# Projection weights on ScalarE's queue, later stores of rotated parts, squares on ScalarE and a new attention order in a two-layer hybrid kernel

## The chip, the cores and the metric

The kernel runs on one core of a Trainium2 chip. The metric is the device time of one execution in microseconds (us); the time before is the median of three executions.

## What is computed

The reference takes 1024 latent tokens of width 1024 (on a grid 64 wide), 256 context tokens and conditioning vectors, and returns the latent stream after two layers. All is float32. Cut to what matters here:

```
layer 0:  u = LN0(h)*(1+scale)+shift            # adaptive values: matrix x conditioning vector
          conv path:  three 512-column projections of u, a gated convolution of width 3
          attention:  q, k = u @ w_qk, rotated by 2-D rotary angles; keys also from 256 context rows
                      4 heads, each (softmax(q1 k1') - lam*softmax(q2 k2')) @ v
                      each head's output o is scaled by rsqrt(mean(o*o) + eps)
          h = LN(alpha*h + gate * ([conv, attention] @ w_out)),  then a squared-ReLU MLP
layer 1:  grouped 2-D Fourier mixing, then a squared-ReLU MLP
```

## The kernel before

A float32 product is made from three matmuls (`mm3`, L87 to L89): each operand is kept as a rounded high part and a low part, the remainder. `split` makes them: a cast on ScalarE (L97) for the high part, a subtraction on VectorE or GpSimd (L98) for the low part. The program's engine order is the order in which the Python code issues instructions; each engine runs its own list in order and waits on semaphores where it needs another's result. A tile from a pool has as many buffers as `bufs` says, and its next use waits until the old one is read. In the built program the DMAs issued by SyncE (SP) and ScalarE take eight semaphores in turn, counted over both engines, and each DMA waits until the one eight before it has landed.

The span of the profiled execution falls into these stretches:

- 0 to 107 us: modulations and the value projection.
- 107 to 265 us: the eight q/k projections. Each loads one weight tile of 128x1024 (512 KB, tag `wraw`, two buffers) with `w_load`, makes its parts `wh` and `wl` with `w_parts`, and multiplies two blocks of 512 columns (for K also one of 256, the context). A pair of projections (A, B) gives one rotated result: `rotate` (L413) combines both blocks with cosine and sine tables on VectorE, GpSimd and ScalarE and makes four parts `rp0` to `rp3` (tags with two buffers), which are stored in DRAM (`Qd`, `Kd`) for the attention to read. `store(*keep)` issues the stores waiting in a list until as many are left as it has arguments.
- 265 to 401 us: twelve conv projections (c = 0 to 11), with weights from the same series: projection i calls `next_weights(i)`, which loads the weights of i+2 and splits those of i+1. So a conv weight loaded late holds up the split behind it.
- Among both runs `Ada`, the adaptive values: eight loads `wa` from `in_ada_w` (L152, SP) for each of eight units, a VectorE instruction on each, and at the end of a unit a load of `in_ada_b` (L177).
- 401 to 672 us: attention. Sixteen pairs of query tiles (four pairs for each of four heads) go through a pipeline in which each step has a number in the table `PIPE`; sorting (number + pair) gives one order for all engines. The steps: S scores of a tile and a half c (PE, L614 to L618; c = 0 and 1 use different k tiles), M row maximum (VectorE L621), E exponential (ScalarE L626), CB, PD, PE the combination of both softmaxes (VectorE L631, GpSimd L635 and L638), T transposes of two key blocks (PE L652), H and L the parts of the transposed weights (ScalarE L658, VectorE L663), P six matmuls into `po` (mm3), OC copy of `po` to `OT` (ScalarE L675), SQ squares (GpSimd L680), SS sums of the squares (PE, L684), SC their use (VectorE). `po` has one buffer in PSUM.
- 672 to 2394.5 us: output projection, layer norms, MLPs and Fourier mixing.

Of the kernel before, what the change touches and what calls it, by code (L numbers as in the profile page):

```python
# [13 lines left out]
F32R = mybir.dt.float32r  # L14
AF = mybir.ActivationFunctionType
ALU = mybir.AluOpType
# [4 lines left out]
P = 128  # L21
# [9 lines left out]
FS = 1.0 / math.sqrt(1024.0 * 128.0)  # L31


def raw(ap):
    return ap.bitcast(F32)


def body(tc, nc, I, O, dbg=None):
# [10 lines left out]
    def popen(name, **kw):  # L49
        p = tc.alloc_tile_pool(name=name, bufs=kw.pop("bufs", 1), **kw)  # L50
        pools[name] = p
        return p

    def pclose(*names):
        for n in names:
            pools.pop(n).release()
# [39 lines left out]
    def split(hi, lo, src, eng=None):  # L96
        a = nc.scalar.copy(hi, src)  # L97
        return a, (eng or nc.vector).tensor_tensor(out=lo, in0=src, in1=raw(hi), op=ALU.subtract)  # L98
# [115 lines left out]
    wsrc = [I["w_qk"][i] for i in range(8)] + [I["w_cv"][i] for i in range(12)]  # L214
    wraws, wtiles = {}, {}

    def w_load(i):
        if i < len(wsrc):
            wraws[i] = pW.tile([P, D], F32, name="wraw", tag="wraw")
            nc.sync.dma_start(out=wraws[i], in_=wsrc[i])  # L220

    def w_parts(i):
        if i < len(wsrc):
# [137 lines left out]
    def store(*keep):  # L361
        while len(stores) > len(keep):
            for o, i in stores.pop(0):
                nc.sync.dma_start(out=o, in_=i)
# [36 lines left out]
    def next_weights(i):  # L401
        w_load(i + 2)
        if i:
            w_parts(i + 1)
# [6 lines left out]
        return ps  # L411

    def rotate(pR, ada, pA, pB, c, dst, scale):  # L413
        parts = [pR.tile([P, 512], F32R, name=f"rp{i}", tag=f"rp{i}", bufs=2) for i in range(4)]
        t = [pR.tile([P, 512], F32, name=f"rt{i}", tag=f"rt{i}") for i in range(4)]
        nc.vector.tensor_tensor(out=t[0], in0=pA, in1=cosT[:, c], op=ALU.mult)
        nc.vector.tensor_tensor(out=t[2], in0=pB, in1=sinT[:, c], op=ALU.mult)
        nc.vector.tensor_tensor(out=t[1], in0=pA, in1=sinT[:, c], op=ALU.mult)
        nc.vector.tensor_tensor(out=t[3], in0=pB, in1=cosT[:, c], op=ALU.mult)
        nc.gpsimd.tensor_tensor(out=t[0], in0=t[0], in1=t[2], op=ALU.subtract)  # L420
        nc.gpsimd.tensor_tensor(out=t[1], in0=t[1], in1=t[3], op=ALU.add)
        ada.tick()
        for i in range(2):
            if scale is None:
                split(parts[i], parts[2 + i], t[i])
            else:
                nc.scalar.mul(parts[i], t[i], scale)
                nc.vector.scalar_tensor_tensor(out=parts[2 + i], in0=t[i], scalar=scale, in1=raw(parts[i]),
                                               op0=ALU.mult, op1=ALU.subtract)
        return [(dst[:, i, :, c], raw(parts[i])) for i in range(4)]  # L430
# [51 lines left out]
    heads = {}  # L482
# [29 lines left out]
    pR = popen("pR", bufs=2, side="left", **tile_waits)  # L512
    pAda = popen("pAda", side="left", **tile_waits)
    with tc.manual_schedule(engines={mybir.EngineType.PE, mybir.EngineType.DVE, mybir.EngineType.Activation,
                                     mybir.EngineType.Pool, mybir.EngineType.SP}):
        w_load(2)
        cosT = pR.tile([P, N], F32, name="cosT", bufs=1)
        sinT = pR.tile([P, N], F32, name="sinT", bufs=1)
        nc.sync.dma_start(out=cosT, in_=I["rope_cos"])
        nc.sync.dma_start(out=sinT, in_=I["rope_sin"])  # L520
        ada = Ada(pAda, ada0[:4])
        for hp in range(2):
            for which in range(2):
                iA = hp * 4 + which * 2
                if iA:
                    next_weights(iA)
                blks = [(UH[b], UL[b], 512) for b in range(2)] + [(CH, CL, NC)] * which
                psA = []
                for blk in blks:
                    psA.append(proj(iA, *blk))  # L530
                    ada.tick(2)
                next_weights(iA + 1)
                dst = (Kd if which else Qd)[hp]
                for b, blk in enumerate(blks):
                    pB = proj(iA + 1, *blk, "tr")
                    if b < 2:
                        st = rotate(pR, ada, psA[b], pB, slice(b * 512, b * 512 + 512), dst, None if which else 0.125)
                    else:
                        parts = [pR.tile([P, 512], F32R, name=f"rp{i}", tag=f"rp{i}", bufs=2) for i in range(4)]
                        split(parts[0][:, :NC], parts[2][:, :NC], psA[b][:, :NC])  # L540
                        split(parts[1][:, :NC], parts[3][:, :NC], pB[:, :NC])
                        st = [(dst[:, i, :, N:NK], raw(parts[i][:, :NC])) for i in range(4)]
                    stores.append(st)
                    store(0)
                    ada.tick()
        ada.tick(len(ada0) * KT)
        ada.end()
        store()
        pclose("pAda", "pR", "pUc")
        pC = popen("pC", bufs=1, side="right", **tile_waits)  # L550
        cb = [pC.tile([P, 514], F32, name=f"cb{i}") for i in range(2)]
        for b in range(2):
            nc.gpsimd.memset(cb[b][:, 0:1], 0.0)
        ada = Ada(popen("pAda", side="right", **tile_waits), ada0[4:])
        pHv = None
        for c in range(12):
            i = 8 + c
            cv = Conv(c)
            next_weights(i)
            for b in range(2):  # L560
                cv.Y(b)
            for b in range(2):
                ps = proj(i, UH[b], UL[b], 512, ("mm", "tr")[b])
                ada.tick(2)
                cv.V(b, ps)
                cv.O(b)
                store(0)
            if c == 7:
                ada.tick(len(ada0) * KT)
            if c == 8:  # L570
                ada.end()
                pclose("pAda")
                popen("pHqL", side="left", **tile_waits)
                pHv = popen("pHv", bufs=2, side="left", **tile_waits)
                load_set(0)
                load_v(0)
                load_set(1)
        store()
# [61 lines left out]
    class Pair:  # L640
# [34 lines left out]
            nc.scalar.copy(heads[self.h]["OT"][:, self.qp * 256:(self.qp + 1) * 256], self.po[:, 0:256])  # L675

        def SQ(self):
            oc = heads[self.h]["OT"][:, self.qp * 256:(self.qp + 1) * 256]
            self.sq = pA.tile([P, 256], F32, name="sq", tag="sq", bufs=1)
            nc.gpsimd.tensor_tensor(out=self.sq, in0=oc, in1=oc, op=ALU.mult)  # L680

        def SS(self):
            for j in range(2):
# [145 lines left out]
    for n in range(3, 8):  # L829
        m = n - 3  # L830
# [4 lines left out]
    for h in range(4):  # L835
        k = PIPE["SC",] + 4 * h + 3
        at(k + 0.001, lambda h=h: finish_stats(h))
        if h < 3:
            for m in range(4):
                base = k + 0.6 + m // 2 * 0.8  # L840
                fr = base + (PIPE["FR",] - base) % 1.0
                fs, fl = (fr + PIPE[o,] - PIPE["FR",] for o in ("FS", "FL"))
                for t, f in ((fr, finish_rows), (fs, finish_split), (fl, finish_low)):
                    at(t + 0.0001 * m, lambda f=f, h=h, m=m: f(h, m))
                written[h] = fl + 0.001
# [360 lines left out]
    T = tail["T"]  # L1206
# [237 lines left out]


PIPE = {
    ("X",): -9.6372,
    ("FR",): -9.5434,
    ("FS",): -8.8084,
    ("FL",): -7.9375,  # L1450
    ("S", 1, 0): 0.0000,
    ("M", 1, 0): 0.3034,
    ("S", 0, 0): 0.3526,
    ("E", 1, 0): 0.4332,
    ("M", 0, 0): 0.4777,
    ("S", 1, 1): 0.5700,
    ("E", 0, 0): 0.6075,
    ("M", 1, 1): 0.6724,
    ("S", 0, 1): 0.7592,
    ("CB", 0): 0.7920,  # L1460
    ("E", 1, 1): 0.8163,
    ("PD", 0): 0.8428,
    ("M", 0, 1): 0.8874,
    ("E", 0, 1): 1.0180,
    ("PE", 0): 1.0297,
    ("CB", 1): 1.1548,
    ("PD", 1): 1.2721,
    ("PE", 1): 1.3784,
    ("T", 0): 1.6732,
    ("H", 0): 1.7224,  # L1470
    ("L", 0): 1.7858,
    ("T", 1): 1.8624,
    ("H", 1): 1.9242,
    ("L", 1): 1.9812,
    ("T", 2): 2.0461,
    ("P", 0): 2.0852,
    ("H", 2): 2.0977,
    ("P", 1): 2.1431,
    ("L", 2): 2.1548,
    ("T", 3): 2.2197,  # L1480
    ("H", 3): 2.2690,
    ("L", 3): 2.3292,
    ("P", 2): 2.3511,
    ("T", 4): 2.4089,
    ("H", 4): 2.4660,
    ("L", 4): 2.5231,
    ("P", 3): 2.5684,
    ("P", 4): 2.7576,
    ("OC",): 2.8491,
    ("SQ",): 2.8874,  # L1490
    ("SS",): 2.9515,
    ("SC",): 2.9891,
}

PERM = np.concatenate([np.arange(512), [512], 1024 - np.arange(1, 512)])
# [109 lines left out]
```

## Time and profile before

| what | value |
|---|---|
| median of three executions | 2397.02 us (2391.02 to 2400.21) |
| profiled execution, own time | 2396.29 us |
| its span | 2394.5 us |
| mean granted TensorE clock | 0.968 |
| busy in the span | PE 2220.9 us (93%), VectorE 1255.8 (52%), GpSimd 1025.7 (43%), ScalarE 695.3 (29%) |

The page gives the busy time of each engine, and for slices of the span the granted TensorE clock as a share of full speed. A timeline gives single instructions, with the idle time of the engine ahead of them and what ended it. DMA share is the mean busy share of the core's 16 DMA engines.

### The profile page before, as it was taken

The page shows a single profiled execution, that of the slowest core. Times are in us where ns is not written, and L with a number is a line of the kernel's source. Part 1 is how long each engine was busy: PE and PEld are TensorE (multiplying, and loading weights), DVE is VectorE, ACT ScalarE, POOL GpSimd, SP SyncE. Part 2 cuts the span into 40 slices and gives each one's busy share as a digit, 9 for nine tenths or more (in the row PEclk, how much of TensorE's full clock was granted, in tenths as well). Part 3 has the DMA queues.
Part 4 walks back from the last instruction along what each step waited for, and adds up shares of the span by engine and source line. Part 5 has one row for each costly group of instructions (what it writes and reads, how often), then busy time and mean ns, then how long its engine had stood idle before and what let it go on. Part 6 is the DMA issues. An engine that isn't in the chain of part 4 may idle for free.

```text
span 2394.5 us, 26145 instructions
## 1 busy us (share of the span) xinstructions
PE 2220.9 (93%) x9978; PEld 1791.4 (75%) x9978; DVE 1255.8 (52%) x1751; ACT 695.3 (29%) x1039; POOL 1025.7 (43%) x704
## 2 busy tenths in 40 slices
PE   7988697887888999999999999898999999999998
PEld 3766585777777877777788887666787888888886
DVE  7545562677545676665443434646544334434335
ACT  5311111666535221112222213435421121121122
POOL 3432222777625433233356643737634233233241
PEclk9998898999899999999999999999999999999999
DMA  7344538354146343332223313345311111111111
GB/s 297 142 149 143 187 127 220 81 128 116 45 123 209 111 157 116 110 115 94 87 97 106 127 49 111 128 156 180 106 61 45 44 54 44 49 49 44 53 44 70
DMA packets 121869, 261.98 MB, mean 109 GB/s; under 512 B 14642, under 2 KB 44594, under 8 KB 121488
## 3 DMA queue, kind: packets, MB, share of 16 engines
q1 hardware_dynamic: 120704, 254.69, 32.8%
q0 software_dynamic: 1040, 5.62, 0.7%
q8 instruction: 78, 1.28, 0.2%
q14 instruction: 47, 0.39, 0.1%
HBM read 213.06 MB, written 47.21 MB: 109 GB/s over the span
## 4 chain that ended last, share of the span: by engine, by line
PE 61%; DMA 12%; POOL 8%; DVE 8%; issue 5%; ACT 2%; SPq 2%; POOLq 0%; DVEq 0%; ACTq 0%
PE bky L87 10%; PE bky L88 10%; PE bky L89 9%; PE bkh L89 8%; PE bkh L88 8%; PE bkh L87 8%; DMA wa<-in_ada_w 3%; DVE aacc L160 2%; DMA wa<-in_ada_b 1%; DMA Kd<-rp 1%; DMA k<-Kd 1%; PE pj L89 1%; PE pj L87 1%; PE pj L88 1%; POOL ra L889 1%
## 5 line engine op out<-in xcount | busy, mean ns | idle before, releaser
L1014 DVE TENSOR_TENSOR acc<-bky,acc 128x512 f32<-128x512 f32 x448 | 304.4, 688 | 323.7 <-PE bky L89 323.1
L87 PE MATMUL bky<-wh,hh 128*128 128x512 f32 x1024 | 404.6, 396 | 18.8 <-DVE acc L1014 15.6
L88 PE MATMUL bky<-wl,hh 128*128 128x512 f32 x1024 | 403.6, 394 | 0.0
L89 PE MATMUL bky<-wh,hl 128*128 128x512 f32 x1024 | 402.2, 393 | 0.0
L998 POOL TENSOR_TENSOR hl<-r,hh 128x512 fp32r<-128x512 f32 x128 | 179.0, 1401 | 409.0 <-DVE r L997 400.0
L961 ACT CAST wh<-wraw 128x1024 fp32r<-128x1024 f32 x128 | 131.4, 1049 | 677.2 <-PE bky L89 482.0
L962 POOL TENSOR_TENSOR wl<-wraw,wh 128x1024 fp32r<-128x1024 f32 x56 | 137.5, 2460 | 303.2 <-ACT wh L961 303.2
L997 DVE TENSOR_TENSOR r<-r 128x512 f32<-128x512 f32 x128 | 118.5, 932 | 243.8 <-ACT hh L996 240.1
L87 PEld LDWEIGHTS bky<-wh,hh 128*128 128x128 f32 x1024 | 193.5, 189 | 70.1 <-DVE acc L1014 22.8
L88 PEld LDWEIGHTS bky<-wl,hh 128*128 128x128 f32 x1024 | 193.6, 189 | 43.3 <-issue 0.7
L89 PEld LDWEIGHTS bky<-wh,hl 128*128 128x128 f32 x1024 | 193.6, 189 | 42.7
L88 PE MATMUL bkh<-UB,wh 128*128 128x512 f32 x512 | 201.1, 393 | 0.7 <-POOL UB L133 0.7
L87 PE MATMUL bkh<-UB,wh 128*128 128x512 f32 x512 | 200.8, 393 | 0.0
L89 PE MATMUL bkh<-UB,wl 128*128 128x512 f32 x512 | 200.8, 393 | 0.0
L960 POOL TENSOR_TENSOR wraw<-wraw,gateg 128x1024 f32<-128x1024 f32 x64 | 156.0, 2439 | 97.8 <-DMA wraw<-in_w 90.3
L87 PE MATMUL bkh<-UA,wh 128*128 128x512 f32 x448 | 177.9, 397 | 0.0
L88 PE MATMUL bkh<-UA,wh 128*128 128x512 f32 x448 | 176.3, 394 | 0.0
L89 PE MATMUL bkh<-UA,wl 128*128 128x512 f32 x448 | 175.7, 394 | 0.0
L160 DVE SCALAR_TENSOR_TENSOR aacc<-wa,cs,aacc 128x512 f32<-128x512 f32 x140 | 143.7, 1027 | 37.5 <-DMA wa<-in_ada_w 35.2
L87 PE MATMUL pj<-UH,wh 128*128 128x512 f32 x320 | 132.5, 414 | 33.1 <-ACT wh L97 33.1
L962 DVE TENSOR_TENSOR wl<-wraw,wh 128x1024 fp32r<-128x1024 f32 x72 | 117.0, 1632 | 81.1 <-ACT wh L961 81.0
L995 ACT ACTIVATE r<-bkh 128x512 f32<-128x512 f32 x120 | 70.7, 595 | 294.8 <-PE bkh L89 283.5
(386 smaller groups left out, 4252.2 us busy)
## 6 DMA issues: line engine op xcount, KB each, us to landing
wraw<-in_w SPq DMA_DIRECT2D x128, 512.0 KB
wa<-in_ada_w SPq DMA_DIRECT2D x160, 256.0 KB
xt<-in_ada_w SPq DMA_DIRECT2D x16, 512.0 KB
xt<-in_x SPq DMA_DIRECT2D x16, 512.0 KB
acc<-Hd SPq DMA_DIRECT2D x16, 512.0 KB
wraw<-in_w_cv SPq DMA_DIRECT2D x12, 512.0 KB
aa<-Ad SPq DMA_DIRECT2D x16, 384.0 KB
k<-Kd SPq DMA_DIRECT2D x16, 320.0 KB
```

What stands on the lines that cost most here:

```text
L87: nc.tensor.matmul(ps, aH, bH, start=start, stop=False)
L88: nc.tensor.matmul(ps, aH, bL, start=False, stop=False)
L89: nc.tensor.matmul(ps, aL, bH, start=False, stop=stop)
L160: nc.vector.scalar_tensor_tensor(out=acc[0], in0=wa, scalar=cs[:, k, 0:1], in1=acc[0], op0=ALU.mult, op1=ALU.add)
L889: nc.gpsimd.tensor_scalar(r, r, 1.0 / D, eps, ALU.mult, ALU.add)
L960: nc.gpsimd.tensor_tensor(out=w, in0=w, in1=g, op=ALU.mult)
L961: nc.scalar.copy(wh, w)
L962: eng.tensor_tensor(out=wl, in0=w, in1=raw(wh), op=ALU.subtract)
L995: nc.scalar.activation(r, ps, AF.Relu)
L997: nc.vector.tensor_tensor(out=r, in0=r, in1=r, op=ALU.mult)
L998: pace[0] = nc.gpsimd.tensor_tensor(out=hl[:, c], in0=r, in1=raw(hh[:, c]), op=ALU.subtract)
L1014: pace[1] = nc.vector.tensor_tensor(out=a[:, c], in0=ps, in1=a[:, c], op=ALU.add)
```

## The change

Four edits. `w_load` issues the weight loads on ScalarE instead of SP. The four `rp` tags get three buffers instead of two, and in the q/k projections the stores of a rotated block are issued two blocks later than its rotation (`store(0, 1)` keeps two entries, `store(0)` kept one); in the conv loop the list is emptied after the first block instead of all but one after each. SQ becomes a Square activation on ScalarE that reads `po` from PSUM, instead of a product on GpSimd that reads `OT`. The table `PIPE` has new numbers, and the four finishing steps FR of a head go in two pairs one period (0.45 for the last) apart instead of all in one place.

```
-            nc.sync.dma_start(out=wraws[i], in_=wsrc[i])
+            nc.scalar.dma_start(out=wraws[i], in_=wsrc[i])
...
-        parts = [pR.tile([P, 512], F32R, name=f"rp{i}", tag=f"rp{i}", bufs=2) for i in range(4)]
+        parts = [pR.tile([P, 512], F32R, name=f"rp{i}", tag=f"rp{i}", bufs=3) for i in range(4)]
...
-                    store(0)
+                    store(0, 1)
...
-                store(0)
+                if not b:
+                    store()
...
         def SQ(self):
-            oc = heads[self.h]["OT"][:, self.qp * 256:(self.qp + 1) * 256]
             self.sq = pA.tile([P, 256], F32, name="sq", tag="sq", bufs=1)
-            nc.gpsimd.tensor_tensor(out=self.sq, in0=oc, in1=oc, op=ALU.mult)
+            nc.scalar.activation(self.sq, self.po[:, 0:256], AF.Square)
...
-                base = k + 0.6 + m // 2 * 0.8
-                fr = base + (PIPE["FR",] - base) % 1.0
+                base = k + 0.6
+                fr = base + (PIPE["FR",] - base) % 1.0 + m // 2 * (1 if h < 2 else 0.45)
...
-    ("P", 3): 2.5684,
-    ("P", 4): 2.7576,
-    ("OC",): 2.8491,
-    ("SQ",): 2.8874,
-    ("SS",): 2.9515,
+    ("P", 3): 2.5668,
+    ("P", 4): 2.7686,
+    ("OC",): 2.8469,
+    ("SQ",): 2.8749,
+    ("SS",): 2.9703,
```

**ScalarE, from the last K rotation into the second conv projection.** Before, casts of weights (`wh`), of rotated parts (`rp`) and copies of the conv gate (`gs`) follow each other:

```order
L97 CAST rp_1727<-rt_1731 128x512
L97 CAST rp_1728<-rt_1732 128x512
L97 CAST rp_1775<-rt_1779 128x512
L97 CAST rp_1776<-rt_1780 128x512
L97 CAST rp_1822<-pj 128x256
L97 CAST rp_1823<-pj 128x256
L97 CAST wh<-wraw 128x1024
L442 COPY gs<-pj 128x512 x2
L97 CAST wh<-wraw 128x1024 x2
```

In the changed program the loads stand among them:

```order
L97 CAST rp_1818<-pj 128x256
L97 CAST rp_1819<-pj 128x256
L220 DMA wraw<-in_w_cv 128x1024
L97 CAST wh<-wraw 128x1024
L442 COPY gs<-pj 128x512 x2
L220 DMA wraw<-in_w_cv 128x1024
L97 CAST wh<-wraw 128x1024
L220 DMA wraw<-in_w_cv 128x1024
L97 CAST wh<-wraw 128x1024
L476 CAST coh_2064<-cy_2023 128x512
L476 CAST coh_2113<-co 128x512
```

The first load here is for conv projection 2, the next for 3 (it stands ahead of the cast of the weights of 2), the last for 4. Each load stands ahead of a cast of other weights, and whatever holds the load up holds up that cast. By the eight semaphores the load for projection 3 waits until the third of the 17 `wa` loads shown below has landed.

**SP, the last stores of K and what follows.** Before:

```order
L177 DMA wa<-in_ada_b 128x512
L364 DMA Kd_961<-rp_1822 4x32x256
L364 DMA Kd_961<-rp_1823 4x32x256
L364 DMA Kd_961<-rp_1824 4x32x256
L364 DMA Kd_961<-rp_1825 4x32x256
L364 DMA G2d_955<-wa 1x512
L152 DMA wa<-in_ada_w 128x512 x7
L220 DMA wraw<-in_w_cv 128x1024
L152 DMA wa<-in_ada_w 128x512 x4
L220 DMA wraw<-in_w_cv 128x1024
```

In the changed program:

```order
L364 DMA Kd_961<-rp_1777 4x32x512
L364 DMA Kd_961<-rp_1818 4x32x256
L364 DMA Kd_961<-rp_1819 4x32x256
L364 DMA Kd_961<-rp_1820 4x32x256
L364 DMA Kd_961<-rp_1821 4x32x256
L364 DMA G2d_955<-wa 1x512
L152 DMA wa<-in_ada_w 128x512 x17
L364 DMA Ad_962<-coh_2064 128x512
L364 DMA Ad_963<-cy_2023 128x512
L152 DMA wa<-in_ada_w 128x512 x4
```

The weight loads are gone from between the `wa` loads. Earlier in this list the stores of the first two Q blocks now stand together behind 22 `wa` loads and the first `in_ada_b` load; before, the first block's stores stood behind 14 `wa` loads.

**PE, the end of one pair of attention.** The names: `s` scores, `pt` transposes, `po` output. Before, the last row of P4, then the scores of c = 1 of a later pair's first tile, the last transposes T1 of the next pair, and SS:

```order
L89 MATMUL po<-ph,vs_2611 128x256
L614 MATMUL s_3256<-k_2614,q 128x512
L615 MATMUL s_3256<-k_2615,q 128x512
L614 MATMUL s_3256<-k_2614,q 128x512
L615 MATMUL s_3256<-k_2615,q 128x512
L617 MATMUL s_3256<-k_2614,q 128x256
L618 MATMUL s_3256<-kx,q 128x256
L652 MATMUL pt<-ident,e_3079 128x128
L652 MATMUL pt<-ident,e_3139 128x128
L652 MATMUL pt<-ident,e_3079 128x128
L652 MATMUL pt<-ident,e_3139 128x128
L684 MATMUL po<-ones,sq 128x1 x2
```

In the changed program the same place:

```order
L619 MATMUL s_3250<-kx,q 128x256
L87 MATMUL po<-ph,vs_2609 128x256
L88 MATMUL po<-pl,vs_2609 128x256
L89 MATMUL po<-ph,vs_2611 128x256
L87 MATMUL po<-ph,vs_2609 128x256
L88 MATMUL po<-pl,vs_2609 128x256
L89 MATMUL po<-ph,vs_2611 128x256
L653 MATMUL pt<-ident,e_3085 128x128
L653 MATMUL pt<-ident,e_3146 128x128
L653 MATMUL pt<-ident,e_3085 128x128
L653 MATMUL pt<-ident,e_3146 128x128
L684 MATMUL po<-ones,sq 128x1 x2
```

The scores stand ahead of P4 now, and P4 directly ahead of T1 and SS. The same exchange was made with P3 and the group of scores before these (S11), so that the order from S11 to SS is S11, P3, T0, S01, P4, T1, SS where it was S11, T0, P4, S01, T1, SS. On ScalarE `sq<-po` stands right behind `OT<-po`, ahead of the next cast `ph<-pt`.

## Rows read from the trace of the kernel before

**Rows 1.** Windows by stage: start:end length, busy of each engine, PEclk, DMA share.

```profile
107.00:265.00 158.00, 131.56 (x584) 106.09 (x582) 70.36 (x89) 20.97 (x31) 42.20 (x26) 0.93 0.45 156
265.00:401.00 136.00, 118.19 (x489) 94.86 (x490) 71.52 (x112) 17.86 (x23) 34.34 (x17) 0.91 0.60 173
401.00:672.00 271.00, 222.41 (x1333) 194.95 (x1331) 174.69 (x255) 153.47 (x247) 178.62 (x104) 0.91 0.42 109
```

**Rows 2.** Waits, 107 to 401 us: sum, times, longest.

```profile
ACT wh L97 <- DMA wraw<-in_w_cv: 58.0, 4, 27.2
...
PE pj L87 <- ACT wh L97: 33.1, 4, 16.0
```

**Rows 3.** Timeline of PE, projections: start, length, instruction, [idle before <- releaser].

```profile
274.80 0.80 PE L87 MATMUL pj<-UH,wh 128*128 128x512 f32 x1 [16.01 <-ACT wh L97]
...
385.45 0.79 PE L87 MATMUL pj<-UH,wh 128*128 128x512 f32 x1 [5.37 <-ACT wh L97]
...
387.89 0.79 PE L89 MATMUL pj<-UH,wl 128*128 128x512 f32 x1 [1.21 <-POOL wl L98]
```

**Rows 4.** Timeline of ScalarE, same stretch.

```profile
174.26 0.37 ACT L97 CAST rp<-pj 128x256 fp32r<-128x256 f32 x1 [9.46 <-DMA Kd<-rp]
...
273.71 1.04 ACT L97 CAST wh<-wraw 128x1024 fp32r<-128x1024 f32 x1 [27.23 <-DMA wraw<-in_w_cv]
...
384.36 1.04 ACT L97 CAST wh<-wraw 128x1024 fp32r<-128x1024 f32 x1 [14.53 <-DMA wraw<-in_w_cv]
```

**Rows 5.** Timeline of SP: DMA issues.

```profile
129.63 3.05 SPq L364 DMA_DIRECT2D Qd<-rp  x4
...
145.30 7.02 SPq L152 DMA_DIRECT2D wa<-in_ada_w  x2
...
235.45 12.13 SPq L364 DMA_DIRECT2D Kd<-rp  x8
...
266.79 0.38 SPq L220 DMA_DIRECT2D wraw<-in_w_cv  x1
...
376.14 0.35 SPq L220 DMA_DIRECT2D wraw<-in_w_cv  x1
```

**Rows 6.** Windows of 10 us in the projections.

```profile
235.00:245.00 10.00, 10.00 (x43) 8.26 (x42) 6.00 (x8) 3.40 (x7) 3.63 (x5) 0.95 0.24 83
380.00:390.00 10.00, 3.41 (x8) 2.23 (x8) 4.76 (x10) 1.04 (x1) 2.35 (x1) 0.64 0.97 249
390.00:400.00 10.00, 10.00 (x39) 8.07 (x39) 0.69 (x1) 0.62 (x1) 1.29 (x1) 0.85 0.13 52
```

**Rows 7.** Waits, 395 to 680 us (attention).

```profile
PE po L684 <- POOL sq L680: 30.3, 14, 3.9
```

**Rows 8.** Timeline of all engines, end of one pair.

```profile
478.32 0.39 PE L614 MATMUL s<-k,q 128*128 128x512 f32 x1
...
481.25 1.33 ACT L626 ACTIVATE e<-s,mx 128x1280 f32<-128x1280 f32 x1 [0.32 <-DVE mx L621]
...
482.56 0.36 ACT L675 COPY OT<-po 128x256 f32<-128x256 f32 x1
482.61 1.34 POOL L635 TENSOR_SCALAR e<-e,ca 128x1280 f32<-128x1280 f32 x1 [3.95 <-DVE ca L632]
...
483.91 0.61 POOL L680 TENSOR_TENSOR sq<-OT 128x256 f32<-128x256 f32 x1
...
484.58 0.61 PE L684 MATMUL po<-ones,sq 128*128 128x1 f32 x4 [2.03 <-POOL sq L680]
```

**Rows 9.** Windows from one SS to the next; the last row sums fifteen.

```profile
469.80:484.60 14.80, 12.77 (x79) 11.69 (x79) 10.19 (x15) 8.92 (x15) 9.00 (x5) 0.88 0.23 72
...
625.25:638.57 13.32, 11.44 (x79) 10.18 (x79) 9.82 (x16) 8.73 (x15) 11.88 (x10) 1.00 0.13 34
...
sum 232.20, PE 196.26 PEld 173.93 DVE 150.04 ACT 131.84 POOL 158.33; mean PE 13.08 PEld 11.60 DVE 10.00 ACT 8.79 POOL 10.56
```

**Rows 10.** Timeline of PE, first scores of the second head.

```profile
461.60 0.51 PE L615 MATMUL s<-k,q 128*128 128x512 f32 x1 [0.61 <-DMA k<-Kd]
```

More of the change, by code (lines that the diff above doesn't have):

```diff
@@ L538, in body @@
                     else:
-                        parts = [pR.tile([P, 512], F32R, name=f"rp{i}", tag=f"rp{i}", bufs=2) for i in range(4)]
+                        parts = [pR.tile([P, 512], F32R, name=f"rp{i}", tag=f"rp{i}", bufs=3) for i in range(4)]
                         split(parts[0][:, :NC], parts[2][:, :NC], psA[b][:, :NC])
@@ L1446 @@
 PIPE = {
[L1447 to L1450, printed above, removed]
+    ("X",): -9.4929,
+    ("FR",): -9.3998,
+    ("FS",): -8.8050,
+    ("FL",): -8.4636,
     ("S", 1, 0): 0.0000,
[L1452 to L1486, printed above, removed]
-    ("P", 3): 2.5684,
-    ("P", 4): 2.7576,
-    ("OC",): 2.8491,
-    ("SQ",): 2.8874,
-    ("SS",): 2.9515,
-    ("SC",): 2.9891,
+    ("M", 1, 0): 0.2941,
+    ("S", 0, 0): 0.3538,
+    ("E", 1, 0): 0.4136,
+    ("M", 0, 0): 0.4648,
+    ("S", 1, 1): 0.5556,
+    ("E", 0, 0): 0.6083,
+    ("M", 1, 1): 0.6665,
+    ("S", 0, 1): 0.7573,
+    ("CB", 0): 0.7790,
+    ("E", 1, 1): 0.8101,
+    ("PD", 0): 0.8210,
+    ("M", 0, 1): 0.8683,
+    ("PE", 0): 0.9265,
+    ("E", 0, 1): 1.0305,
+    ("CB", 1): 1.1562,
+    ("PD", 1): 1.1981,
+    ("PE", 1): 1.3036,
+    ("T", 0): 1.6698,
+    ("H", 0): 1.7234,
+    ("L", 0): 1.7761,
+    ("T", 1): 1.8716,
+    ("H", 1): 1.9437,
+    ("L", 1): 1.9965,
+    ("T", 2): 2.0547,
+    ("P", 0): 2.1013,
+    ("H", 2): 2.1082,
+    ("L", 2): 2.1610,
+    ("P", 1): 2.1633,
+    ("T", 3): 2.2254,
+    ("H", 3): 2.2790,
+    ("L", 3): 2.3317,
+    ("P", 2): 2.3651,
+    ("T", 4): 2.4272,
+    ("H", 4): 2.4807,
+    ("L", 4): 2.5335,
+    ("P", 3): 2.5668,
[3 more added lines that the diff above has]
+    ("SS",): 2.9703,
+    ("SC",): 3.0068,
 }
```

## Prediction

> **What bounds the kernel now.** I read the windows by stage first, since a share of the whole span hides the stages. TensorE (PE) is busy 131.56 of 158 us while q and k are projected, 118.19 of 136 us in the conv projections and 222.41 of 271 us in attention [rows 1]. So 26.4, 17.8 and 48.6 us of PE idleness, 92.8 in all, are what this change can reach, besides the clock: it was granted at 0.91 to 0.93 there. What comes behind 672 us isn't touched.
>
> Next the waits of 107 to 401 us. PE stood 33.1 us in four waits for a cast of weights, and ScalarE's casts stood 58.0 us for conv weights to land [rows 2]. The timeline of PE says where: 16.01 us ahead of the matmuls at 274.80 (conv projection 2) and 5.37 ahead of those at 385.45 (projection 11) [rows 3]. ScalarE had been free for 27.23 and 14.53 us at these places, with the weights' DMA as the releaser [rows 4]. The reader is to look at SP then: its list stands 12.13 us in eight stores of K from 235.45, and the weight load that PE will need is issued at 266.79 only [rows 5]. While these stores run, the DMA engines are 0.24 busy and move 83 GB/s [rows 6]: about 4 of 16 engines run. The late load is late because SP's list is, not for want of DMA engines.
>
> In attention the waits name one thing: PE's SS waited 30.3 us in 14 of 16 pairs for the squares on GpSimd [rows 7]. The timeline of one pair's end shows the chain: scores S11 start at 478.32, E11 at 481.25, OC copies `po` at 482.56, but GpSimd has just begun a 1.34 us product (PD) at 482.61, the squares come at 483.91 and take 0.61, and SS starts at 484.58 after 2.03 us [rows 8]. From one SS to the next it is 14.80 us in this pair and 13.32 in the quickest; the mean of fifteen is 232.20/15 = 15.5, with PE 13.08, VectorE 10.00, ScalarE 8.79 and GpSimd 10.56 busy [rows 9].
>
> **The change part by part.**
>
> Weight loads on ScalarE and later stores, 107 to 300 us. The loads leave SP's list. The load for conv projection 2 no longer stands behind the stores; but ScalarE must issue the load for projection 3 ahead of the cast for 2, and that load waits until the third `wa` load behind all K stores has landed. So the end of the stores still decides. Their bytes: 32 stores of 256 KB and 8 of 128 KB, 9.4 MB, at 83 GB/s 113 us. They start at 129.63 now; in the new order they stand behind loads that were issued up to about 145.30 [rows 5]. I put the start at 146, and 146+113 = 259, with some holes 262, about the place where they end now (the weight load at 266.79 stands behind them and seven `wa` loads). Three `wa` loads then take some 4 us, the cast 1.04 and the step to PE 0.05: PE goes on at about 268 in place of 274.80. **Gain 7.** Bounds: the stores end as soon as their bytes allow or the loads aren't held, 259 or a little less, gain 15; they end 12 us later, having started 16 later, loss 5. The third buffer of `rp` removes waits such as the 9.46 us of ScalarE at 174.26 [rows 4]; ScalarE and VectorE have cover there (ScalarE 20.97 busy of 158 [rows 1]), so its worth is in the holes between the stores and is within the term. Issuing 20 loads on ScalarE, 0.35 to 0.38 us each on SP [rows 5], is 7 us of a mostly idle engine: 0; if the cover were gone in the first stage, where two casts of weights now stand ahead of activations that PE waits for, 2 us.
>
> Last conv weight. SP issued it at 376.14 behind the loads of q, k and v [rows 5]; on ScalarE it is issued as soon as its buffer is free, two projections ahead. The wait of 5.37 and the following one of GpSimd's low part (the matmul at 387.89, idle 1.21) go [rows 3]. And the clock: 8 matmuls took 3.41 us of PE in the window from 380 with 0.64 granted, 39 took ten at 0.85 [rows 6]; at full clock the second is 8.5, the first some 1.8, so 3.1 us more. 5.4+1.2+3.1 = 9.7, less some 0.7 for the loads of q and k, which then meet the weight. **Gain 9**; bounds 0 (the load merely waits for a semaphore behind those transfers) to 10.
>
> Squares on ScalarE and the new order. The nearest row for the square is OC, the same 128x256 read of PSUM by the same engine, 0.36 us; bounds 0.3 and GpSimd's 0.61. ScalarE rises from 8.79 to 9.15 a pair, far below PE's 13.08: its cover is large, and GpSimd loses 0.61. In the old order PE had from S11's start to SS 484.58-478.32-2.03 = 4.23 us of work [rows 8], that is 7680 matmul columns (S 2560, T 512, P 1536 each), 0.55 ns a column. One P more makes 5.1 us. The chain on the other side: OC came 4.24 us behind S11's start; half of OC and the square (0.26+0.36) and a hand-over of some 0.1 give 4.95. But OC now also waits for P4, with only T1 (0.3 to 0.6) between P4 and SS, so I leave 0.5 us a pair. 30.3-14x0.5 = 23. Bounds: 30, if it all goes; 8, if the copy is held up behind exponentials each time (1.33+0.2 us, 14 times 21 of the 30 left).
>
> What comes with it: at 0.88 a pair has 12.77 us of PE, at 1.00 it has 11.44 [rows 9], 1.33 more; eight of the first thirteen windows read less than 1, five of them 0.88 or 0.89. At 1.33 to 1.8 each (the 1.8 is my estimate for the slower windows) that is 11 to 14 us. Whether these drops follow from SS's idle 2 us the rows don't settle (pairs at 1.00 had waits too). I take about half, 7; bounds 0 and 14. And what is late next: the k tiles of a head. The second head's first scores waited 0.61 us for them already [rows 10]. With a pair 1.5 us shorter and the scores one P (0.8) earlier, each of three head changes loses about 2.3: 7 us; bounds 0 and 15. Together **23** in attention, 10 to 45. Check: 15.5-1.5 = 14.0 a pair, still above the quickest of before, 13.32.
>
> Sum: 7+9+23 = 39 from the profiled execution's 2396.3 (0.7 below the median): **2357**.
>
> One rule of the Trainium skill speaks against the first two terms: page "DMA: Bandwidth & Descriptors", section "Issuing engines are not separate DMA queues", says that DMAs of several issuing engines end up on the same 16 DMA engines and that issuing in parallel saves only the sequencer's time. By it the sum would lose the first two terms, as in the first rival. The trace agrees in that stores use a quarter of the engines, which every load shares; but what stood here was the sequencer, for 12 us at a time.
>
> **The rivals.**
>
> (a) The weights come no earlier: ScalarE's loads share the DMA engines on which the stores run, and stand at their semaphores until SP's transfers land. For it: the load for projection 3 waits for SP's loads as said; against it: 83 GB/s of traffic while PE starves. Then only attention gains: 2396-23 = 2373. The skill's section above gives this.
>
> (b) Attention gains little: the squares come early, but PE meets the exponentials (score buffers), k loads or GpSimd instead. For it: GpSimd has 10.56 us a pair, and the pairs at full clock still had about two idle us of PE. Gain 6 there: 2396-16-6 = 2374.
>
> (c) Slower: ScalarE stands in order at a weight load that waits for stores, while the casts that make the next stores stand behind it. The place is the two conv loads during the second q/k pair; each time the store series would run dry, once for eight stores of 256 KB at 83 GB/s (25 us). Two such holes and the start 16 us later are 66 late; with the two other gains, 2396+66-9-23 = 2430. It decides once the delay is above 9+23 = 32, so the stores end later than 262+32 = 294. Against it: the loads wait for stores eight DMAs back, and the casts behind them take a few us, with a third buffer between.
>
> (d) It doesn't do what it says: the loads wait as before, and SQ, behind OC on the same engine, ends when GpSimd's did. About 2394. Against it: the order of ScalarE puts nothing between OC and SQ.
>
> **How the numbers follow.** Chances: forecast 0.50, (a) 0.15, (b) 0.20, (c) 0.07, (d) 0.08. The forecast's own range is 2326 (15, 10 and 45 gained) to 2380 (2 lost early, 6 late, 12 in attention). The range for 8 in 10 takes in (a) and (b) with their own spread: 2328 to 2392. A measurement of this kernel tells about 0.5%, 12 us, from no change. Faster than 2385: the forecast, (a) and most of (b), 0.82; within: (d) and the rest of (b), 0.11; slower than 2409: (c), 0.07.
>
> **What would show it.** Stores: the last K store issued near 260, PE's wait at conv projection 2 below 10 us, and no wait at projection 11; ScalarE's own loads issued within a few us of the casts. Attention: SS's wait below 0.8 us a pair, from SS to SS about 14.0, PE's clock at 1.00 in more pairs, waits for k of 2 to 3 us at three head changes. I am wrong if the stores end beyond 275, if another wait of PE in attention (for exponentials, for GpSimd) sums to more than 15 us, or if stages behind 672 us move.

## The result and the profile after

The changed kernel takes 2363.43 us (median of four, 2360.19 to 2365.24) against 2394.02 before: ratio 0.987, 95% interval 0.984 to 0.990, so 30.6 us or 1.3% faster. Forecast was 2357. The profiled execution has a span of 2363.5 us.

Windows by stage of the changed kernel, as in [rows 1] (length, busy time of PE, PEld, VectorE, ScalarE, GpSimd, PEclk, DMA share, GB/s):

```profile
107.00:265.00 158.00, 130.33 (x578) 105.70 (x576) 68.39 (x88) 20.78 (x30) 42.25 (x26) 0.91 0.47 160
265.00:401.00 136.00, 121.01 (x513) 97.76 (x513) 78.43 (x121) 23.70 (x32) 39.59 (x20) 0.94 0.69 195
401.00:672.00 271.00, 228.80 (x1406) 197.88 (x1407) 206.24 (x274) 160.62 (x275) 173.15 (x94) 0.97 0.39 101
```

The fixed windows no longer cut at stages, since all comes earlier, and the third now takes in some of the output projection. The stages are read from their marks: the last copy of the conv projections (L476 on ScalarE) starts at 386.68 instead of 401.95, 15.3 us earlier. That compares one execution of each kernel; the account below compares several. The sums SS run from 423.37 to 642.0 us, 218.6 us, in place of 232.2 [rows 9].

The timeline of PE, projections, against [rows 3]:

```profile
215.23 0.80 PE L87 MATMUL pj<-UH,wh 128*128 128x512 f32 x1 [7.55 <-ACT wh L97]
...
217.99 0.79 PE L89 MATMUL pj<-UH,wl 128*128 128x512 f32 x1 [1.53 <-POOL wl L98]
...
268.71 0.80 PE L87 MATMUL pj<-UH,wh 128*128 128x512 f32 x1 [12.73 <-ACT wh L97]
...
271.20 0.80 PE L89 MATMUL pj<-UH,wl 128*128 128x512 f32 x1 [1.26 <-POOL wl L98]
```

Conv projection 2 restarts at 268.71 instead of 274.80. At projection 11 there is no wait any more, and this one of the kernel before is gone too:

```profile
178.19 0.79 PE L87 MATMUL pj<-UH,wh 128*128 128x512 f32 x1 [9.25 <-ACT wh L97]
```

But there is a new one at 215.23, the eighth q/k projection. The timeline of ScalarE shows what ended both:

```profile
213.70 0.33 ACTq L220 DMA_DIRECT2D wraw<-in_w_cv  x1
214.13 1.05 ACT L97 CAST wh<-wraw 128x1024 fp32r<-128x1024 f32 x1 [10.83 <-DMA wa<-in_ada_w]
...
267.22 0.35 ACTq L220 DMA_DIRECT2D wraw<-in_w_cv  x1
267.61 1.04 ACT L97 CAST wh<-wraw 128x1024 fp32r<-128x1024 f32 x1 [21.88 <-DMA wa<-in_ada_w]
```

Each time ScalarE had stood at the issue of a weight load (L220) for the landing of a `wa` load that SP issues, and a cast of other weights stood behind. SP's timeline shows where these `wa` loads were:

```profile
192.70 13.16 SPq L364 DMA_DIRECT2D Kd<-rp  x8
205.97 1.73 SPq L152 DMA_DIRECT2D wa<-in_ada_w  x1
...
258.18 1.35 SPq L364 DMA_DIRECT2D G2d<-wa  x1
259.62 21.73 SPq L152 DMA_DIRECT2D wa<-in_ada_w  x17
```

The one of 205.97 stands behind eight stores of K, those of 259.62 behind all of them.

In attention, the waits of the changed kernel from 395 to 660 us:

```profile
PE po L87 <- DVE ss L692: 16.5, 12, 1.7
...
PE s L615 <- ACT e L627: 12.1, 8, 8.1
...
PE po L684 <- ACT sq L680: 6.3, 14, 0.8
...
PE s L616 <- DMA k<-Kd: 1.5, 3, 0.7
```

Lines behind SQ have moved by a few numbers against the kernel before. SS waits 6.3 us where it waited 30.3 [rows 7]. A new wait is the largest: P0, the first P of a pair, waits 16.5 us for L692, the last instruction of SC, where it waited 0.8 before. Of the 12.1 us behind exponentials 8.1 stand at the start of attention, where it was 7.1. The windows of one pair and of the whole stretch from the first SS to the last, against [rows 9]:

```profile
464.65:477.36 12.71, 11.29 (x79) 10.14 (x79) 11.23 (x16) 8.64 (x16) 9.58 (x6) 1.00 0.49 139
423.37:642.00 218.63, 184.79 (x1202) 162.45 (x1202) 174.69 (x225) 133.69 (x230) 149.33 (x78) 0.98 0.44 110
```

A pair without head change takes 12.71 us. Over the stretch, PE is idle 218.63-184.79 = 33.8 us; before it was 232.20-196.26 = 35.9. So the idle time hardly fell, and 11.5 of the 13.6 us are matmuls that run quicker at a higher granted clock: 0.98 over this stretch in place of 0.92, with 13 of the 15 windows at 1.00 in place of 6. The timeline of one pair's end, against [rows 8], shows why the idle time came back:

```profile
463.94 0.37 ACT L676 COPY OT<-po 128x256 f32<-128x256 f32 x1 [0.43 <-PE po L89]
464.20 0.39 ACT L680 ACTIVATE sq<-po 128x256 f32<-128x256 f32 x1
...
464.65 0.61 PE L684 MATMUL po<-ones,sq 128*128 128x1 f32 x4 [0.31 <-ACT sq L680]
464.81 2.92 POOL L639 TENSOR_TENSOR e<-e,e 128x1280 f32<-128x1280 f32 x1
...
465.11 0.69 DVE L664 TENSOR_TENSOR pl<-pt,ph 128x512 fp32r<-128x512 f32 x1 [0.39 <-ACT ph L659]
...
465.71 2.03 DVE L691 SCALAR_TENSOR_TENSOR ss<-R 128x2 f32<-128x2 f32 x1
...
467.85 0.16 DVE L692 SCALAR_TENSOR_TENSOR ss<-po,ss 128x2 f32<-128x2 f32 x1
...
468.06 0.39 PE L87 MATMUL po<-ph,vs 128*128 128x256 f32 x1 [1.11 <-DVE ss L692]
```

OC, square and SS follow each other within 0.7 us. GpSimd, which has no square to do, begins its 2.92 us product at 464.81. VectorE's L691, an instruction on 128x2 values, starts at 465.71 and takes 2.03 us: it ends at 467.74, when GpSimd's product does (464.81+2.92 = 467.73). L692 behind it releases PE's P0 at 468.06. The sixteen L691 of attention took 2.0 us in the mean, as the view by groups has it (busy us, mean ns, idle before):

```profile
L691 DVE SCALAR_TENSOR_TENSOR ss<-R 128x2 f32<-128x2 f32 x16 | 32.0, 2002 | 0.0
```

In the kernel before they were short, since ten of the sixteen met GpSimd's 0.61 us square and not its long product (shortest, median and longest in ns; the mean is 470):

```profile
L691 DVE SCALAR_TENSOR_TENSOR ss<-R x16: 148/163/2841, 439.1 to 665.7; 128x2 f32<-128x2 f32 x16
```

Of the changed kernel's sixteen, fourteen overlap a GpSimd instruction, and each of these ends 0.01 to 0.03 us behind it. The last two, with GpSimd idle, took 0.15 us:

```profile
626.87 0.15 DVE L691 SCALAR_TENSOR_TENSOR ss<-R 128x2 f32<-128x2 f32 x1
```

### The profile page after: what moved, and what is told of

The parts are those of the page before. It is cut to its first block, busy times and chain, and to the rows that moved or that the text cites. A ratio compares the mean times of both kernels' runs of the same rounds, so it can differ in the third digit from the quotient of the medians.

```text
span 2363.5 us, 26175 instructions
## 1 busy us (share of the span) xinstructions
PE 2209.3 (93%) x9978; PEld 1781.6 (75%) x9978; DVE 1273.8 (54%) x1751; ACT 697.2 (30%) x1055; POOL 1019.0 (43%) x688
## 4 chain that ended last, share of the span: by engine, by line
PE 65%; DVE 8%; DMA 8%; POOL 7%; issue 5%; ACT 3%; SPq 2%; ACTq 0%; POOLq 0%; DVEq 0%
PE bky L87 10%; PE bky L88 10%; PE bky L89 10%; PE bkh L88 8%; PE bkh L89 8%; PE bkh L87 8%; DMA wa<-in_ada_w 3%; PE pj L89 2%; PE pj L87 2%; PE pj L88 2%; DVE aacc L160 2%; SPq L364 1%; DMA k<-Kd 1%; POOL ra L889 1%; DVE ss L691 1%
```

## The experiments

All ratios are to the kernel before on the same chip; differences in us are of medians, and the recorded ratios give up to 5 us more or less. Differences to the changed kernel are between sets of runs taken apart, in which the kernel before took 2391.57 to 2394.18 us.

**1. The loads alone, and with the later stores.** Edit of the first against the kernel before; the second has the edits to `bufs` and to `store` as well.

```
-            nc.sync.dma_start(out=wraws[i], in_=wsrc[i])
+            nc.scalar.dma_start(out=wraws[i], in_=wsrc[i])
```

> The kernel before with the weight loads on ScalarE alone (stores, squares and order as before). Theory A (the list of SP held the loads up, the later stores and third buffers add little): conv projection 11 no longer waits and projection 2 restarts near 268 us, so some 14 us off, about 2380. Theory B (the gain before 401 us needs the later stores too, since ScalarE's casts of rotated parts stand at the two-buffer limit and now also behind weight loads): only the 9 us of projection 11, about 2385, or less if ScalarE's list holds the casts up.

> The kernel before with the loads on ScalarE, the third buffers and the later stores; squares and attention order as before. Theory A and B alike: all of the gain before 401 us, 15 to 16 us (the conv projections' last matmuls end 16 us earlier in the changed kernel), about 2378 to 2380. If the parts are not independent, the time is off 2394 less 16 by more than 4.

Loads alone: 2372.47 against 2394.18, ratio 0.9922 (0.9900 to 0.9944), 21.7 us faster. With the later stores: 2381.96, 0.9948 (0.9931 to 0.9966), only 12.2. So the loads alone did better than both theories had, and the later stores took 9.5 back (6 by the ratios). The timelines of PE, at conv projection 2 above all, with the loads alone and then with the later stores:

```profile
175.99 0.80 PE L87 MATMUL pj<-UH,wh 128*128 128x512 f32 x1 [8.16 <-ACT wh L97]
...
263.81 0.79 PE L87 MATMUL pj<-UH,wh 128*128 128x512 f32 x1 [7.56 <-ACT wh L97]
```

```profile
273.38 0.80 PE L87 MATMUL pj<-UH,wh 128*128 128x512 f32 x1 [12.57 <-ACT wh L97]
```

The timelines of ScalarE and SP with the loads alone:

```profile
262.32 0.34 ACTq L220 DMA_DIRECT2D wraw<-in_w_cv  x1
262.71 1.04 ACT L97 CAST wh<-wraw 128x1024 fp32r<-128x1024 f32 x1 [20.36 <-DMA G2d<-wa]
```

```profile
258.95 0.25 SPq L364 DMA_DIRECT2D G2d<-wa  x1
```

SP issues the last G2d store at 258.95 here, at 262.83 with the later stores and at 258.18 in the changed kernel, which has them too: this place moves by some us between executions, and not one way with the edit. What moved with it is what the load at 262.32 waits for. Here the DMA eight before it is that G2d, with the later stores the third `wa` load behind it. Counted from the issue of G2d, PE restarts 4.9 us later here and 5.5 in experiment 3, which has the same stores; with the later stores it is 10.5 to 10.6 us, in the second kernel here, the changed kernel and that of experiment 5 alike. With the loads on SP it is 11.7 to 13.1 us. The wait of 7.55 at 215 is not there with the loads alone; there is one of 8.16 us at 175.99 instead, which the later stores take away.

**2. Attention alone.** Squares on ScalarE, `PIPE` and the finishing steps as in the change; loads and stores as before.

> The kernel before with the squares on ScalarE and the new order of attention; loads and stores as before. If the two halves of the change add up: 15 us off, about 2379, TensorE waiting some 16 us for the sums' last step (L692 on VectorE) and 6 for the squares. If the attention gain hangs on the earlier loads (k tiles, weights), less than 8 off.

2371.08, ratio 0.9925 (0.9900 to 0.9949), 23.1 us faster (18 by the ratio); SS waited 6.3, P0 16.4 us for the same last step of SC, as in the changed kernel. From the first SS to the last it is 217.4 us in place of 231.9, both to the start of the last. Attention's part doesn't hang on the loads.

**3. Without the later stores.** The changed kernel with `store(0)`, two `rp` buffers and the old store call in the conv loop; these three were only run together.

> The changed kernel with the stores and the rp buffers as before (stores one block late, two buffers), so the loads on ScalarE and the attention part alone. Theory A (the later stores cost time: they start 16 us later and end later, and TensorE's restart at conv projection 2 waits for their end): the two gains add up, 22 from the loads and 18 to 23 from attention, 2350 to 2354, ten below the changed kernel; conv projection 2 restarts near 264 us in place of 268.7. Theory B (the later stores cost nothing, the difference between loads alone and loads with later stores is the spread of executions): within 4 of 2363.

2355.35 against 2393.26, ratio 0.9845 (0.9825 to 0.9864): 8 us below the changed kernel (6 by the ratios), with PE restarting at 266.25. Theory A nearly holds in its number, not in its reason: G2d is issued at 260.78 here, in the changed kernel at 258.18, so the later stores didn't end later there. The two single parts sum to 44.8, both together gave 37.9; by the ratios it is 36.6 and 37.1, so a loss where they meet isn't shown.

**4. The square and the order by themselves.** In attention, against the kernel before: SQ as an activation alone, and `PIPE` with the finishing steps alone.

> The kernel before with the squares on ScalarE alone, order of attention as before (OC, then the square, ahead of the last cast; scores still ahead of SS by S01 and T1). Theory A (the square behind GpSimd's product was the whole of SS's wait): SS's wait falls from 30 to under 10 us, and 10 to 15 us go, about 2381. Theory B (the new order is what lets the square be early, since OC stands behind the exponential E11): SS's wait stays above 18 us, less than 8 us gained.

> The kernel before with the new order of attention alone, squares on GpSimd. Theory A: SS still waits for GpSimd, which now does the product and the square behind OC; the later P4 makes OC later, so SS's wait grows to 30 us or more and nothing is gained, 2390 to 2400. Theory B: the order gives one P more between S11 and SS (0.8 us a pair), so SS's wait falls by some 12 us and about 10 are gained.

The square alone: 2379.78, ratio 0.9941 (0.9925 to 0.9958), 13.5 faster. The order alone: 2377.53, 0.9936 (0.9913 to 0.9960), 15.7. Waits of the first, whose lines L691, L683 and L679 are the changed kernel's L692, L684 and L680, then of the second:

```profile
PE po L87 <- DVE ss L691: 12.2, 8, 1.7
...
PE po L683 <- ACT sq L679: 10.2, 14, 1.2
```

```profile
PE po L684 <- POOL sq L680: 25.6, 14, 4.1
...
PE po L87 <- DVE ss L692: 3.4, 4, 0.9
```

The square on ScalarE takes SS's wait from 30.3 to 10.2 us, and lets GpSimd start early, so that 12.2 us come back at P0. With the order alone SS still waits 25.6 us, 4.7 less, and yet 16 us are gained; I had expected either no gain or 12 less of waiting. The traces show where part of the rest lies. From the start of the first SS to that of the last, the kernel before takes 231.9 us with PE busy for 195.9 at a granted clock of 0.92. With the order alone it is 221.6 us, PE busy for 190.4 at 0.95: 10.3 us less, of which 5.5 are quicker matmuls. The other 5 of the 15.7 don't show in attention. What lies before and behind it, which the edit doesn't touch, is 12 us shorter in this profile than in that of the kernel before, by the spread of executions. With the square alone it is 222.3 us, PE busy for 185.0 at 0.99: the idle time is 37.3 us in place of 35.9, so its whole gain there is quicker matmuls. Neither theory named this. Why the clock is granted more isn't shown; the sum of PE's idle time didn't fall.

**5. L691 somewhere else.** The changed kernel with the instruction taken out of SC and put ahead of the next pair's CB:

```
+        def RR(self):
+            q = slice(self.qp * 2, self.qp * 2 + 2)
+            r0 = heads[self.h]["R"][:, q, 0]
+            d = heads[self.h]["ss"][:, q]
+            nc.vector.scalar_tensor_tensor(out=d, in0=r0, scalar=SUB_EPS, in1=r0, op0=ALU.mult, op1=ALU.mult)
+
         def SC(self):
...
-            nc.vector.scalar_tensor_tensor(out=d, in0=r0, scalar=SUB_EPS, in1=r0, op0=ALU.mult, op1=ALU.mult)
...
+        at(PIPE["CB", 0] + p + 0.9999, pairs[p].RR)
```

> The changed kernel with the one instruction L691 (128x2, eps times the square of the softmax sums) taken out of SC and put ahead of the next pair's CB, where GpSimd stands idle and waits for VectorE; the same work. Theory A (L691 has two SBUF inputs and is held until GpSimd's running e+e product ends, and P0 of the next pair stands behind it): L691 falls from 2.0 to 2.6 us to about 0.15, TensorE's wait of 16.5 us for L692 goes to under 3, and some 12 to 16 us go: about 2349. Theory B (L691 is long because of a dependence on its own inputs, or the wait for L692 is only a shift of a wait that other engines set): L691 stays above 1 us at the new place or another wait of TensorE takes over, and the time stays within 4 of 2363.

2354.68 against 2394.18, ratio 0.9846 (0.9824 to 0.9868), 8.8 us below the changed kernel. Groups of instructions, the waits and the window from the first SS to the last of this kernel:

```profile
L691 DVE SCALAR_TENSOR_TENSOR ss<-R 128x2 f32<-128x2 f32 x16 | 3.3, 208 | 0.0
```

```profile
PE s L615 <- ACT e L627: 11.4, 7, 8.4
...
PE po L684 <- ACT sq L680: 6.8, 14, 1.3
```

```profile
426.80:635.90 209.10, 189.75 (x1202) 165.44 (x1202) 146.21 (x223) 134.79 (x230) 149.07 (x78) 0.97 0.47 116
```

One of them in the timeline, and what GpSimd does there:

```profile
465.75 0.15 DVE L691 SCALAR_TENSOR_TENSOR ss<-R 128x2 f32<-128x2 f32 x1
...
466.38 1.33 POOL L636 TENSOR_SCALAR e<-e,ca 128x1280 f32<-128x1280 f32 x1 [0.61 <-DVE ca L633]
```

GpSimd has idled 0.61 us and waits for VectorE's `ca` behind it. The same instruction on the same values takes 0.21 us in the mean instead of 2.00, and the wait for L692 is gone from the list. The longest of the sixteen, 1.07 us, stands inside a GpSimd product and ends with it. Theory A holds for the cause. It gave 12 to 16 us, and the idle time did fall by that: 209.10-189.75 = 19.4 instead of 33.8. But PE's busy time rose from 184.8 to 189.8 us at a granted clock of 0.97 instead of 0.98, which took 5 back.

**6. Wide stores.** The changed kernel, and then the kernel before, with

```
-                nc.sync.dma_start(out=o, in_=i)
+                if len(o.shape) == 3:
+                    for g in range(4):
+                        nc.sync.dma_start(out=o[g], in_=i[g * 32:g * 32 + 32])
+                else:
+                    nc.sync.dma_start(out=o, in_=i)
```

> The changed kernel with each store of a rotated part issued as four DMAs of 32 rows, one for each of the outer dimension's four entries: same bytes, four times the issues. Theory A (a store with outer dimension 4 runs on about 4 of 16 DMA engines, and the series of 9.4 MB decides when SP's list comes free): the DMA share in the stores rises above 0.5, SP's stores no longer hold its list for 11 to 17 us at a time, TensorE's waits of 7.55 us at 215 and 12.73 us at 268.7 fall to under 3 each, and 12 to 20 us go, about 2347. Theory B (the stores are bound by issue, by landing latency or by their producers): the waits stay within 4 us of what they are and the time within 5 of 2363, or above it since SP issues 120 DMAs more.

> The kernel before with the stores issued as four DMAs of 32 rows each, nothing else changed (weight loads on SP, old attention). Theory A (SP's list was late because the stores ran on a quarter of the DMA engines): the waits at conv projection 2 (16.0) and at 178 us (9.3) fall by half or more and 12 to 20 us go, so the loads' move to ScalarE and the wide stores mend the same thing in two ways; about 2378. The wait at projection 11 (5.4 us) stays, since its load stands behind the loads of q, k and v. Theory B (the loads have to leave SP's list all the same, since the issues fill it): less than 6 gained.

On the changed kernel: 2343.05 against 2393.26, ratio 0.9783 (0.9759 to 0.9808), 20 us below it. Two stretches of stores in the changed kernel, and two with wide stores:

```profile
192.00:206.00 14.00, 10.54 (x38) 8.05 (x39) 9.88 (x15) 2.52 (x4) 5.91 (x4) 0.67 0.37 124
240.00:258.00 18.00, 15.98 (x71) 12.91 (x69) 0.69 (x1) 0.88 (x2) 0.91 (x1) 1.00 0.30 114
```

```profile
186.00:202.00 16.00, 13.67 (x61) 10.97 (x62) 13.74 (x16) 4.51 (x6) 9.05 (x6) 0.89 0.63 161
231.00:247.00 16.00, 16.00 (x71) 12.95 (x69) 0.69 (x1) 1.05 (x1) 2.40 (x1) 1.00 0.50 143
```

The DMA share goes from 0.30 to 0.37 up to 0.50 to 0.63, and PE's waits at 215 and 268.7 us are gone. Two things were not as expected. SP's list is held as long as before, now by issues:

```profile
147.85 15.14 SPq L366 DMA_DIRECT2D Qd<-rp  x32
```

And a new wait appears, PE at the end of an adaptive unit, behind VectorE's sum over `wa` loads:

```profile
258.46 2.07 PE L174 MATMUL ag<-aacc,ones 128*128 128x512 f32 x2 [11.44 <-DVE aacc L160]
...
275.05 0.50 PE L89 MATMUL pj<-UH,wl 128*128 128x512 f32 x1 [1.18 <-POOL wl L98]
```

On the kernel before: 2374.85 against 2391.57, ratio 0.9924 (0.9903 to 0.9946), 16.7 faster. PE is at conv projection 2 some 16 to 20 us earlier (four profiles with narrow stores and the loads on SP have 270.2 to 274.8), but the wait there hardly fell (16.01 [rows 3]; 12.9 to 13.6 in the other three):

```profile
254.36 0.79 PE L87 MATMUL pj<-UH,wh 128*128 128x512 f32 x1 [14.54 <-ACT wh L97]
```

So both theories are right in part: the stores' width sets when the q/k projections come through, but a weight load on SP's list is late behind them at either width.

**7. Both repairs.** Wide stores and L691 moved, on the changed kernel; and the same with the stores one block late and two buffers.

> The changed kernel with both: L691 ahead of the next pair's CB, and the stores as four DMAs each. The two act in different stretches, so 9 and 20 us add up: about 2334. If TensorE's wait behind VectorE's sums at 258 us or the start of attention takes some back, 2334 to 2342.

> The same as the kernel with L691 moved and four DMAs for each store, but with the stores one block late and two rp buffers as before. Theory A (the later stores cost time because narrow stores need the time; with wide stores the order matters little): within 5 of the kernel with later stores. Theory B (later stores cost because the adaptive loads and the stores change places on SP's list): 5 to 8 faster, about 2328.

2329.62 (ratio 0.9741, 0.9719 to 0.9763) and 2328.14 (0.9735, 0.9711 to 0.9758), against 2391.57: 62 and 63 us faster than before, 34 and 35 below the changed kernel. The two repairs' 8.8 and 20.4 make 29, and the intervals are too wide to call the rest a gain of its own. With wide stores the medians don't differ by when the stores are issued, as theory A said, though the two profiles do: PE waits 11.51 us behind VectorE's sum over `wa` loads with the later stores, 4.04 with the early ones. Windows of the second from 107 us:

```profile
107.00:265.00 158.00, 150.74 (x679) 123.19 (x678) 87.67 (x125) 25.29 (x36) 50.52 (x31) 0.97 0.65 200
265.00:401.00 136.00, 123.34 (x570) 100.33 (x569) 78.81 (x117) 39.13 (x58) 54.45 (x27) 0.95 0.58 161
```

PE is busy 150.74 of 158 us where it had 130.33 in the changed kernel.

## Why the prediction was right, and where not

**Weight loads and later stores (7 forecast).** Conv projection 2 restarts at 268.71, forecast 268, and ScalarE waited there for the third `wa` load, as worked out. The number is luck, in two ways. First, this place moves by several us between executions. Kernels with the instructions of the kernel before up to attention restart at 274.80, 270.21, 270.21 and 271.30 (the kernel before, experiments 2 and 4), kernels with the changed ones at 268.71, 273.38 and 270.19 (the changed kernel, experiments 1 and 5): in the mean 271.6 and 270.8. So the gain here was near 1 us. With the loads alone, at 263.81 and 266.25, it was 6.6. Second, two misses cancel in 268.71. G2d behind the stores was issued at 258.18, sooner than the 262 put for the stores' end. But "Three `wa` loads then take some 4 us" failed: ScalarE's load was issued at 267.22, 9.0 us behind G2d, and 9.0 to 9.1 in both other profiles.

The other step that failed is "its worth is in the holes between the stores and is within the term": the later stores have a price of their own, 8 us (experiment 3) to 9.5 (experiment 1), 6 by the ratios. They change which DMA is the eighth before a weight load, and trade the wait at 178 us for one at 215. So the 7 left out a loss nearly as large as the gain. The prediction's sign, a wait below 10 us at projection 2, did not come: it was 12.73. At this place rival (a), weights no earlier, is nearly what happened. Rival (c) named the mechanism of the wait at 215 and the place, a weight load in the second q/k pair that waits behind stores; it happened once, for 7.55+1.53 us on PE, not twice for 25.

**Last conv weight (9).** This term was right. No wait is left at projection 11. From the restart at projection 2 to the last copy of the conv projections it is 9.2 us less (117.97 in place of 127.15), a granted clock of 0.97 in place of 0.94 included; in the means of the profiles just named it is 117.8 in place of 127.5.

**Squares and order (23).** SS's wait: 24.0 us less, forecast 23. The granted clock: 11.5 us less of PE busy time, forecast 7, bound 14. The k tiles: 1.5 us of waits in place of 0.6, forecast 7 more. These three would have made 34.6. The step that failed is "and what is late next: the k tiles of a head". Late next was VectorE's L691 and with it SC and P0: 16.5 us where the kernel before had 0.8. By the prediction's own sign, another wait of PE above 15 us, that part was wrong. I had followed the copy and the square up to SS, but not SC, which P0 needs since `po` has one buffer; and I had taken the 0.61 us off GpSimd as pure gain, while that square had mostly kept GpSimd's long product out of L691's way. The rest of the difference, some 5 us between first and last SS, lies in smaller waits that I haven't followed. Rival (b) had the right shape, a new wait in attention that eats much of the gain, but not the path: GpSimd holds PE up by way of VectorE.

**The sum.** 39 forecast, 30.6 measured, with an interval of 24 to 38. In the one pair of profiles shown above it is 15.3 before attention, forecast 16, and 13.6 from the first SS to the last, forecast 23. Over the profiles with equal instructions in a stretch it is 10.6 before attention (the last copy at 388.6 in the mean of three, 399.1 in that of four; experiment 1 has 12.2 in time), and 15.5 from the first SS to the last (217.4 and 232.8, four each). So both parts gave about two thirds of their forecast, and the agreement of the first in the shown pair is the spread of executions. These 26 us lie within the interval. Behind the last SS nothing was changed; that stretch takes 1721.5 us in this profile, 1723.0 before, and 1714 to 1721 in the profiles of experiments 1 to 5. The rule of the Trainium skill ("DMA: Bandwidth & Descriptors", "Issuing engines are not separate DMA queues") would have had the loads' move save only the sequencer's time, usually small; experiment 1 shows 21.7 us. What was saved is indeed the sequencer's, as the section has it, but it isn't small here: SP's list, held for 11 to 17 us at a time, was what the loads had to leave.

## What to carry to other kernels

When a wait of one engine on another is taken away, follow the data to the next use of the same single buffer, here from SS over SC to P0; and ask what the relieved engine will now run, and against whom. When DMAs of two engines share semaphores in turn, each change in the number or order of DMAs on one list changes what the other list waits for, so read for each load which DMA stands eight before it. Before a few us at one place of a trace are booked to a change, read the same place in other executions with the same instructions: here it moved by 5 us. And look at how many DMA engines a transfer uses before moving transfers about: on the kernel before, the wide stores alone gave 16.7 us and the loads' move alone 21.7.

## What the runs showed of the hardware

A VectorE instruction with two inputs in SBUF was held for as long as a GpSimd product on SBUF ran: L691 on 128x2 values took 2.03 us, ending with GpSimd's at 467.7, and all fourteen that overlap GpSimd in the changed kernel end 0.01 to 0.03 us behind it; with GpSimd idle it took 0.15. L664, with one input in PSUM, ran its 0.69 us at 465.11 inside the same product, and 34 of its kind inside GpSimd instructions took no longer than those outside (0.69 in the mean). The Trainium skill says so in "SBUF — State Buffer", section "SBUF: two separate sides": VectorE and GpSimd share a pair of ports, and a VectorE instruction with two SBUF inputs and a GpSimd instruction that reads SBUF take it whole, whichever starts first. The trace agrees, and the prediction would have been better with it.

A store with an outer dimension of 4 left the DMA engines 0.24 to 0.37 busy; the same bytes as four DMAs of 32 rows had them 0.50 to 0.63 busy, at 143 to 161 GB/s in place of 83 to 124 in stretches of stores. Their issues then held SP's list, at 15.14/32 = 0.47 us each.

The granted TensorE clock from the first SS to the last was 0.92 in the kernel before and 0.98 in the changed one, and PE's work there took 11.5 us less (184.79 and 196.26; 196.26x0.92/0.98 = 184.2). With the square alone it was 0.99 although PE's idle time was no shorter.
